# Later transposes, later gate products and a later start of v's preparation in a decoder step on one core

## The chip, the core and the metric

The kernel runs on one core of one Trainium2 chip. The metric is the device time of one execution in microseconds (us), as the median of several runs. The engines are TensorE (PE, with its weight loads PEld), VectorE (DVE), ScalarE (ACT), GpSimd (POOL) and SyncE (SP); the last three also issue DMAs.

## The reference, cut to what matters

One layer of a hybrid decoder works on 256 prompt tokens and 8 sample tokens, all in fp32. After two mixers and a norm (x1), 16384 experts of one neuron each are added (PEER). The change lies in this part:

```python
q = (xt @ w_q).reshape(n_pad, PEER_HEADS, 2, PEER_DKEY // 2)
s1 = einsum('thd,hkd->thk', q[:, :, 0], keys1); s2 = einsum('thd,hkd->thk', q[:, :, 1], keys2)
t1, i1 = top_k(s1, 16); t2, i2 = top_k(s2, 16)
cand = t1[..., :, None] + t2[..., None, :]           # 16 x 16 pairs of keys
top, pos = top_k(cand, 16)                           # 16 experts per head and token
gate = softmax(top)
hid = gelu(einsum('td,thkd->thk', xb, u_tab[ib]))    # u rows of the chosen experts
out = einsum('thk,thkd->td', gate * hid, v_tab[ib])  # v rows of the chosen experts
x2 = layer_norm(ALPHA * x1 + out)                    # then y = x2 + sigmoid(x2 @ wg) * (p @ wp)
```

## The kernel before

208 of the 264 tokens are treated densely: all 16384 neurons are computed for them as matrix products, and a gate matrix that is zero but for the chosen experts selects. The other 56 tokens are treated sparsely: the rows of their experts are gathered by indirect DMA (112 gathers of 128 rows, 1 MB each), and VectorE multiplies them with x1 (`ug`, L1365) or adds them up (`x1s`, L1375): these are called gather products here.

**The stages around the change.** The u stage makes the hidden values of 128 blocks of 128 experts (`pair_block` with `u_evac`, results to `a_d` in DRAM); the v stage makes 8 x 16 blocks that sum over the experts (`pair_block` with `v_evac`, sums in the tiles `acc`). A block is two *halves*; each half takes one half megabyte of weights. SyncE fetches them a block at a time into `w` (3 buffers), ScalarE rounds them to `whi` (L158), VectorE takes the rest `wlo` (L159), 5 buffers each, and TensorE multiplies by both: 16 matrix products in a half (L293 and L296 with `whi`, L294 with `wlo`).

**The order of the work.** The kernel writes its instructions out engine by engine from a small scheduler that runs while the program is built. After every half, `tick` is called once. It first runs functions that `defer(n, fn)` put n ticks later, and then the background tasks, which are generators: `yield x` spends x of the tick's budget, `yield ("w", n)` waits n ticks, and `Grid` keeps steps a fixed number of ticks apart. A tick has no length in time: it says only behind which half an instruction stands in its engine's queue. Each engine takes its queue in order. Halves and ticks are counted here from the start of the u stage; halves 0 to 255 are u, 256 to 511 are v.

**The tasks that the change touches.**
- `select_all`: chooses the experts for three groups of tokens (`select`, on VectorE, with the result `sel`: index parts and gates). For the two dense groups TensorE transposes `sel` into the bank `slt`, and ScalarE copies that into `slot`.
- `gates(t0, n)`: for four tokens a step, GpSimd (three tokens) and VectorE (one) make a one-hot row `o1` with the gate in it, and ScalarE makes `o2`. Six ticks later `g_mm` multiplies them on TensorE (bank `gps`, 4 products in fp32, eight records of the trace; called a gate product here) and ScalarE copies the result to the tile `gs`. Every eight steps, ScalarE's queue stores `gs` (2 MB) to `g_d` in DRAM. 20 steps belong to the first group, 32 to the second.
- `to_v`, called once when all gates are done and nothing is deferred: it closes the pools of selection and gates, opens the pool `vp` in the same memory, and spawns `prep(0)` and `residual`. `residual` copies x1 into the 16 tiles `acc` (ScalarE, two copies a tick). `prep(c)` makes the coefficients for one eighth of the v stage, in four parts: GpSimd's queue loads gates (`gl`) and hidden values (`al`), VectorE multiplies them (`al`, two instructions), ScalarE rounds (`co`), VectorE takes the rest (`co`). `gl` and `al` have two buffers. The v stage needs `prep(0)` done: the first half reads parts 0 and 1, the second parts 2 and 3.

In the program before, the first transposes stand behind half 53, the gate steps run from tick 55 to 210, `to_v` comes at tick 218, and the last gather product stands at tick 488. When sparse work is done, `folded` adds its last result (bank `yS`, 4 pieces on TensorE), and `Norm.rest` makes the sample part of the second norm beside the last eighth of v.

Of the kernel before, what the change touches and what calls it, by code (L numbers as in the profile page):

```python
# [18 lines left out]
PT = 256  # L19
# [26 lines left out]
NB, TR = divmod(TD, TB)  # L46
# [5 lines left out]
def hybrid_step(ctx: ExitStack, tc: tile.TileContext, xT, pT, w_in, w_dt, w_bs, w_bc, w_o, w_q, w_pg, w_pp,  # L52
                uT, vP, uR, vR, keysT, par, hpar, hist, h0, eye, tri, iota, fold, yT, o_hp, o_hs, o_cp, o_cs, o_sp, o_ss):
    nc = tc.nc
    te, ve, ac, gp, sy = nc.tensor, nc.vector, nc.scalar, nc.gpsimd, nc.sync
# [50 lines left out]
    def bank(name, tag="bg", bufs=4):  # L106
        return psum.tile([128, 512], F, name=name, tag=tag, bufs=bufs)
# [4 lines left out]
    ident = cpool.tile([128, 128], F, name="ident")  # L112
# [51 lines left out]
    tasks = []  # L164
    later = []
    clock = {"t": 0, "credit": 0.0, "in": False}

    def defer(n, fn):
        later.append((clock["t"] + n, fn))
# [33 lines left out]
    def spawn(gen, first=False):  # L203
        tk = {"gen": gen, "wait": 0}
        tasks.insert(0 if first else len(tasks), tk)
        return tk
# [864 lines left out]
    g_d = dram.tile([NB, 128, 128, TB], F, name="g_d")  # L1071
    gr_d = dram.tile([128, 128, TR], F, name="gr_d")
    DONE = {}
# [130 lines left out]
    def select_all():  # L1204
        while sum(h in DONE for h in range(PH)) < PH:
            yield ("w", 1)
        t2_stack.close()
        sp = P["sp"] = sp_stack.enter_context(tc.tile_pool(name="select", bufs=1))
        P["oh"] = oh_stack.enter_context(tc.tile_pool(name="onehot", bufs=1))
        for t, (t0, n, nh) in enumerate(TT):  # L1210
            sel = sp.tile([128, 3, nh * TOPK], F, name=f"sel{t}")
            yield from select(t, sel)
            if t < 2:
                send(sel, t, nh)
            if t == 1:
                spawn(sparse_experts(), True)
            if t != 1:
                nd = min(n, TD - t0)
                yield ("w", 2)
                ps = bank("slt")  # L1220
                for q in range(3):
                    te.transpose(ps[:, q * 128:q * 128 + n], sel[:n, q], ident[:n, :n])
                for q in range(3):
                    ac.copy(slot[q][:, t0:t0 + nd], ps[:, q * 128:q * 128 + nd])
                if t == 0:
                    tasks.insert(0, {"gen": gates(t0, nd), "wait": clock["t"] + 1})
        while "G" + str(PT // 2) not in DONE:
            yield ("w", 1)
        yield from gates(0, PT // 2)

# [27 lines left out]
    def gates(t0, n):  # L1258
        oh = P["oh"]
        grid = Grid()  # L1260
        for tt in range(t0, t0 + n, 4):
            b0, q0 = divmod(tt, TB)
            tb = TB if b0 < NB else TR
            if q0 == 0:
                GS["t"] = oh.tile([128, 128, TB], F, name="gs", tag="gs", bufs=2)
            gs = GS["t"].rearrange("p e t -> p (e t)")[:, 0:128 * tb].rearrange("p (e t) -> p e t", t=tb)
            o1 = oh.tile([128, 4, 128], F, name="o1", tag="o1", bufs=3)
            o2 = oh.tile([128, 4, 128], F, name="o2", tag="o2", bufs=3)
            for q in range(4):
                c = slice(tt + q, tt + q + 1)  # L1270
                (gp if q < 3 else ve).tensor_scalar(o1[:, q], iot, slot[0][:, c], slot[2][:, c], OP.is_equal, OP.mult)  # L1271
                ac.activation(o2[:, q], iot, AF.Abs, bias=slot[1][:, c], scale=-1.0)  # L1272
            ac.activation(o2, o2, AF.Relu, bias=1.0, scale=-1.0)
            defer(6, lambda o1=o1, o2=o2, gs=gs, q0=q0: g_mm(o1, o2, gs, q0))
            if q0 + 4 == tb:
                defer(8, lambda gs=gs, b0=b0: ac.dma_start(out=g_d[b0] if b0 < NB else gr_d, in_=gs))
            yield 0.1
            yield grid(3)
        DONE["G" + str(t0)] = True

    def g_mm(o1, o2, gs, q0):
        ps = bank("gps")
        for q in range(4):
            te.matmul(ps[:, q * 128:(q + 1) * 128], o2[:, q], o1[:, q], start=True, stop=True)  # L1284
        ac.copy(gs[:, :, q0:q0 + 4].rearrange("p e t -> p t e"), ps.rearrange("p (t e) -> p t e", e=128))
# [110 lines left out]
    ctx.push(oh_stack)  # L1396
    slot = [tp.tile([128, TD], F, name=f"slot{q}") for q in range(3)]
    spawn(select_all())


# [118 lines left out]
    def to_v():  # L1519
        nonlocal vp  # L1520
        oh_stack.close()
        sp_stack.close()
        tkp_stack.close()
        t1_stack.close()
        vp = ctx.enter_context(tc.tile_pool(name="vp", bufs=1))
        t = spawn(prep(0), True)
        spawn(residual())
        return t

    nxt = None  # L1530
    for e in range(NE):
        pair_block(x1_p, u_evac(e), 1.1)
        if nxt is None and "G0" in DONE and not later:
            nxt = to_v()
    while nxt is None:
        tick(1.2)
        if "G0" in DONE and not later:
            nxt = to_v()
    while len(ACC) < KB:
        tick(1.2)  # L1540
# [2 lines left out]
    for c in range(ECH):  # L1543
        run_out(nxt)
        if c + 1 < ECH:
            nxt = spawn(prep(c + 1), True)
# [151 lines left out]
```

## Time and profile before

| | us |
|---|---|
| median of 3 runs | 2490.54 (2488.34 to 2492.01) |
| the profiled execution | 2492.02 |
| its span, first to last instruction | 2490.2 |
| u stage (1076.6 to 1758.4) | 681.8 |
| v stage (1758.4 to 2374.5) | 616.1 |

Times in the profile count from the first instruction of the profiled execution. A row of the timeline is: start, duration, engine, line, operation, out<-in, shapes, count, and in brackets the idle time before it and what ended that. A row of the waits is: who <- what it waited for, total us, times, longest. A row of a group is: line, engine, operation, out<-in, shapes, count, then busy us, mean ns of one, and the idle time before them. A granted clock of 0.50 is half of TensorE's rate.

### The profile page before, as it was taken

What the parts mean: (1) busy time and instruction counts of PE and PEld (TensorE: products, weight loads), DVE (VectorE), ACT (ScalarE), POOL (GpSimd) and SP (SyncE); (2) the same over time, 40 slices, a digit from 0 to 9 for tenths busy, and PEclk for the clock granted to TensorE, in tenths of its full rate; (3) what the DMA queues carried; (4) which work ended last, traced back from release to release, by engine and by line L of the source; (5) the groups of instructions that cost most, each with busy time, mean ns of one, the idle gap of its engine ahead of it and who ended that gap; (6) DMA issues with size and microseconds to landing.
All of it is one profiled execution on the core that took longest, in us unless ns stands there. A gap on an engine that the chain in (4) does not pass through costs nothing.

```text
span 2490.2 us, 47970 instructions
## 1 busy us (share of the span) xinstructions
PE 2429.0 (98%) x19049; PEld 2403.0 (96%) x19049; DVE 2036.4 (82%) x3296; ACT 1424.4 (57%) x2206; POOL 626.2 (25%) x720
## 2 busy tenths in 40 slices
PE   8998999999999999999999999999999999999989
PEld 8998999999999999998999999999999999999989
DVE  7898976557455578999998777769899989999987
ACT  5656543455444455754677888866544555444564
POOL 2332200000000010100249567642332323322201
PEclk9999999999999999999999999999999999999999
DMA  6788855555555555566679999999999999999554
GB/s 223 245 280 264 284 203 177 199 188 201 189 201 189 201 188 198 198 206 206 227 277 356 371 371 363 361 358 395 392 380 386 383 375 395 374 371 376 192 176 148
DMA packets 137105, 688.91 MB, mean 277 GB/s; under 512 B 15744, under 2 KB 53168, under 8 KB 63280
## 3 DMA queue, kind: packets, MB, share of 16 engines
q1 hardware_dynamic: 89168, 495.46, 55.8%
q0 software_dynamic: 28688, 158.69, 16.4%
q10 hardware_dynamic: 19024, 31.69, 3.4%
q8 instruction: 149, 2.44, 0.4%
q14 instruction: 76, 0.62, 0.1%
HBM read 646.32 MB, written 39.46 MB: 275 GB/s over the span
## 4 chain that ended last, share of the span: by engine, by line
PE 61%; DVE 16%; DMA 10%; issue 7%; ACT 5%; POOL 1%; ACTq 0%; SPq 0%; DVEq 0%; POOLq 0%
PE mm L255 13%; PE mm L257 13%; PE mm L256 13%; PE mm L293 13%; DVE wlo L159 7%; PE mm L294 6%; DMA w<-vP 5%; ACT whi L158 2%; DMA w<-uT 2%; DVE ug L1365 1%; DMA h0t<-h 1%; PE gps L1284 1%; DVE acc L1482 1%; PE mm L296 1%; ACT o L1272 1%
## 5 line engine op out<-in xcount | busy, mean ns | idle before, releaser
L159 DVE TENSOR_TENSOR wlo<-w,whi 128x1024 fp32r<-128x1024 f32 x916 | 1112.6, 1223 | 336.3 <-ACT whi L158 327.9
L158 ACT CAST whi<-w 128x1024 fp32r<-128x1024 f32 x916 | 945.3, 1044 | 648.1 <-DMA w<-vP 228.6
L293 PE MATMUL mm<-x,whi 128*128 128x416 f32 x1920 | 573.1, 365 | 4.5 <-ACT whi L158 4.5
L293 PE MATMUL mm<-co,whi 128*128 128x416 f32 x1920 | 563.3, 362 | 0.0
L257 PE MATMUL mm<-x,wlo 128*128 128x264 f32 x1920 | 533.4, 278 | 12.4 <-DVE wlo L159 12.3
L255 PE MATMUL mm<-x,whi 128*128 128x264 f32 x1920 | 534.5, 278 | 4.7 <-ACT whi L158 4.7
L256 PE MATMUL mm<-x,whi 128*128 128x264 f32 x1920 | 531.9, 277 | 0.0
L294 PE MATMUL mm<-x,wlo 128*128 128x208 f32 x2048 | 504.6, 257 | 10.9 <-DVE wlo L159 10.8
L294 PE MATMUL mm<-co,wlo 128*128 128x208 f32 x2048 | 501.4, 255 | 6.5 <-DVE wlo L159 6.2
L294 PEld LDWEIGHTS mm<-x,wlo 128*128 128x128 f32 x2048 | 393.2, 193 | 18.9 <-DVE wlo L159 18.1
L294 PEld LDWEIGHTS mm<-co,wlo 128*128 128x128 f32 x2048 | 391.3, 192 | 10.9 <-DVE wlo L159 10.8
L257 PEld LDWEIGHTS mm<-x,wlo 128*128 128x128 f32 x1920 | 364.7, 190 | 15.1 <-DVE wlo L159 15.0
L293 PEld LDWEIGHTS mm<-x,whi 128*128 128x128 f32 x1920 | 365.9, 191 | 6.0 <-ACT whi L158 4.8
L255 PEld LDWEIGHTS mm<-x,whi 128*128 128x128 f32 x1920 | 364.9, 190 | 6.3 <-ACT whi L158 4.9
L256 PEld LDWEIGHTS mm<-x,whi 128*128 128x128 f32 x1920 | 364.9, 190 | 0.0
L293 PEld LDWEIGHTS mm<-co,whi 128*128 128x128 f32 x1920 | 364.0, 190 | 0.1
L1271 POOL TENSOR_SCALAR o<-iot,slot,slot 128x128 f32<-128x128 f32 x156 | 200.8, 1294 | 3.0 <-issue 1.2
L1295 POOL DMA_INDIRECT ug<-vR,sidx x56 | 105.2, 1879 | 271.8 <-DVE x1s L1375 212.8
L1295 POOL DMA_INDIRECT ug<-uR,sidx x56 | 94.7, 1691 | 247.1 <-DVE ug L1365 194.6
L1365 DVE SCALAR_TENSOR_TENSOR ug<-ug,x1s 128x2048 f32<-128x2048 f32 x56 | 127.8, 2283 | 2.3 <-DMA ug<-uR,sidx 2.3
L1375 DVE SCALAR_TENSOR_TENSOR x1s<-ug,scf,x1s 128x2048 f32<-128x2048 f32 x53 | 124.3, 2344 | 1.0 <-DMA ug<-vR,sidx 1.0
L898 POOL CAST r1h<-r1gbh 128x2 fp32r<-128x2 f32 x16 | 7.0, 439 | 439.9 <-DVE mxl L242 439.9
(364 smaller groups left out, 3927.1 us busy)
## 6 DMA issues: line engine op xcount, KB each, us to landing
w<-uT SPq DMA_DIRECT2D x128, 1024.0 KB
w<-vP SPq DMA_DIRECT2D x128, 1024.0 KB
w<-w_in SPq DMA_DIRECT2D x118, 1024.0 KB
w<-w_bc SPq DMA_DIRECT2D x16, 1024.0 KB
w<-w_bs SPq DMA_DIRECT2D x16, 1024.0 KB
w<-w_o SPq DMA_DIRECT2D x16, 1024.0 KB
w<-w_q SPq DMA_DIRECT2D x16, 1024.0 KB
w<-w_pg SPq DMA_DIRECT2D x16, 1024.0 KB
```

Source lines behind the costliest of these rows:

```text
L158: ac.copy(hi, w)
L159: ve.tensor_tensor(lo, w, hi.bitcast(F), OP.subtract)
L255: te.matmul(ps, wh, vh, start=(first and q == 0), stop=False)
L256: te.matmul(ps, wh, vl, start=False, stop=False)
L257: te.matmul(ps, wl, vh, start=False, stop=(last and q == n - 1))
L293: te.matmul(ps, hi[:, ws], both, start=(kb == 0), stop=False)
L294: te.matmul(ps[:, :TD], lo[:, ws], one, start=False, stop=False)
L296: te.matmul(ps, hi[:, ws], both, start=False, stop=True)
L1271: (gp if q < 3 else ve).tensor_scalar(o1[:, q], iot, slot[0][:, c], slot[2][:, c], OP.is_equal, OP.mult)
L1295: gp.indirect_dma_start(out=t, out_offset=None, in_=tab, in_offset=bass.IndirectOffsetOnAxis(ap=sidx[:, c:c + 1], axis=0))
L1365: ve.scalar_tensor_tensor(t, t, 1.0, x1s, OP.mult, OP.mult, accum_out=shid[:, c:c + 1])
L1375: ve.scalar_tensor_tensor(x1s, t, scf[:, c:c + 1], x1s, OP.mult, OP.add)
```

## The change

The transposes of `sel` and their copies become a deferred function, five ticks on, in place of a wait of two. The gates of the first group start six ticks after the selection instead of one after the transposes. Gate products are deferred by eight ticks instead of six, the stores by ten instead of eight. Of three steps, every third is four ticks from the next instead of three. And `to_v` waits until seven ticks have passed since gates and deferred work were done. By the scheduler's clock the gate steps now run from tick 58 to 230, the last store stands at tick 240, and `to_v` comes at tick 250, six halves before the end of u. 17 ticks then pass without a half, until `prep(0)` is done.

```diff
@@ select_all
-                yield ("w", 2)
-                ps = bank("slt")
-                for q in range(3):
-                    te.transpose(ps[:, q * 128:q * 128 + n], sel[:n, q], ident[:n, :n])
-                for q in range(3):
-                    ac.copy(slot[q][:, t0:t0 + nd], ps[:, q * 128:q * 128 + nd])
+
+                def to_slots(t0=t0, n=n, nd=nd, sel=sel):
+                    ps = bank("slt")
+                    for q in range(3):
+                        te.transpose(ps[:, q * 128:q * 128 + n], sel[:n, q], ident[:n, :n])
+                    for q in range(3):
+                        ac.copy(slot[q][:, t0:t0 + nd], ps[:, q * 128:q * 128 + nd])
+                    DONE["slot" + str(t0)] = True
+
+                defer(5, to_slots)
                 if t == 0:
-                    tasks.insert(0, {"gen": gates(t0, nd), "wait": clock["t"] + 1})
-        while "G" + str(PT // 2) not in DONE:
+                    tasks.insert(0, {"gen": gates(t0, nd), "wait": clock["t"] + 6})
+        while "G" + str(PT // 2) not in DONE or "slot0" not in DONE:
             yield ("w", 1)
@@ gates
-            defer(6, lambda o1=o1, o2=o2, gs=gs, q0=q0: g_mm(o1, o2, gs, q0))
+            defer(8, lambda o1=o1, o2=o2, gs=gs, q0=q0: g_mm(o1, o2, gs, q0))
             if q0 + 4 == tb:
-                defer(8, lambda gs=gs, b0=b0: ac.dma_start(out=g_d[b0] if b0 < NB else gr_d, in_=gs))
+                defer(10, lambda gs=gs, b0=b0: ac.dma_start(out=g_d[b0] if b0 < NB else gr_d, in_=gs))
             yield 0.1
-            yield grid(3)
+            yield grid(3 + (tt // 4 % 3 == 2))
@@ the u stage
+    def stored():
+        if "G0" in DONE and not later and "stored" not in DONE:
+            DONE["stored"] = clock["t"] + 7
+        return clock["t"] >= DONE.get("stored", 1 << 30)
+
     for e in range(NE):
         pair_block(x1_p, u_evac(e), 1.1)
-        if nxt is None and "G0" in DONE and not later:
+        if nxt is None and stored():
             nxt = to_v()
     while nxt is None:
         tick(1.2)
-        if "G0" in DONE and not later:
+        if stored():
             nxt = to_v()
```

On TensorE, the first transposes stood between halves 53 and 54 (the last products of a half, then `slt`, then the next half):

```order
L294 MATMUL mm<-x_12661,wlo_94 128x208
L293 MATMUL mm<-x_12661,whi_90 128x416
L294 MATMUL mm<-x_12661,wlo_94 128x208 x2
L296 MATMUL mm<-x_12661,whi_90 128x416
L1222 MATMUL slt<-ident,sel_14127 128x128 x3
L293 MATMUL mm<-x_12220,whi_13258 128x416
```

And now, three halves on:

```order
L293 MATMUL mm<-x_12367,whi_92 128x416
L294 MATMUL mm<-x_12367,wlo_95 128x208
L293 MATMUL mm<-x_12367,whi_92 128x416
L294 MATMUL mm<-x_12367,wlo_95 128x208
L1223 MATMUL slt<-ident,sel_14127 128x128 x3
L293 MATMUL mm<-x_12514,whi_91 128x416
```

TensorE has 48 more products ahead of the transposes than before, and the copies to `slot` on ScalarE move with them.

On ScalarE, before, the last store of the gates and the first copies of `residual` (`acc`), with the weights' `whi` between and behind them:

```order
L1276 DMA g_d<-gs 128x4096
L158 CAST whi_91<-w 128x1024
L158 CAST whi_90<-w 128x1024
L1409 COPY as<-mm 128x208
L1501 COPY acc<-x_12220 128x2x2x104 x2
L158 CAST whi_13258<-w 128x1024
```

Now the store stands here:

```order
L1289 COPY gs<-gps 128x4x128
L158 CAST whi_91<-w 128x1024
L158 CAST whi_90<-w 128x1024
L1413 COPY as<-mm 128x208
L1280 DMA g_d<-gs 128x4096
L158 CAST whi_13258<-w 128x1024
```

And the end of u, with the copies, is this:

```order
L158 CAST whi_13258<-w 128x1024
L1413 COPY as<-mm 128x208
L1417 ACTIVATE as<-as 128x416
L1418 DMA a_d<-as 128x416
L1459 CAST co<-al 128x8x104
L1505 COPY acc<-x_12367 128x2x2x104 x4
L1459 CAST co<-al 128x8x104
L1505 COPY acc<-x_12514 128x2x2x104 x4
L1459 CAST co<-al 128x8x104
```

Between store and first copies there were three instructions and are now some twenty, eleven halves' worth; and the last `co` stand behind the last u block's `as`, with no weights between.

On VectorE, before, `prep(0)` (`al`, `co`) stands among the weights of the u stage; a part of it:

```order
L1444 TENSOR_TENSOR al<-al,gl 128x4x192
L1445 TENSOR_TENSOR al<-al,gl 128x4x16
L159 TENSOR_TENSOR wlo_94<-w,whi_90 128x1024
L1375 SCALAR_TENSOR_TENSOR x1s<-ug,scf,x1s 128x2048
L159 TENSOR_TENSOR wlo_13259<-w,whi_13258 128x1024
L1410 TENSOR_TENSOR as<-mm,as 128x208
L159 TENSOR_TENSOR wlo_97<-w,whi_93 128x1024
L1456 TENSOR_TENSOR co<-al,co 128x8x104
```

Now, from the last u block's `as` on:

```order
L1414 TENSOR_TENSOR as<-mm,as 128x208
L1379 SCALAR_TENSOR_TENSOR x1s<-ug,scf,x1s 128x2048
L1460 TENSOR_TENSOR co<-al,co 128x8x104
L1379 SCALAR_TENSOR_TENSOR x1s<-ug,scf,x1s 128x2048
L1448 TENSOR_TENSOR al<-al,gl 128x4x192
L1449 TENSOR_TENSOR al<-al,gl 128x4x16
L1460 TENSOR_TENSOR co<-al,co 128x8x104
L1379 SCALAR_TENSOR_TENSOR x1s<-ug,scf,x1s 128x2048
L1448 TENSOR_TENSOR al<-al,gl 128x4x192
L1449 TENSOR_TENSOR al<-al,gl 128x4x16
L1460 TENSOR_TENSOR co<-al,co 128x8x104
L1379 SCALAR_TENSOR_TENSOR x1s<-ug,scf,x1s 128x2048
```

There is no `wlo` between them any more, and a gather product stands before each part; one more part and one more gather product follow, then the next `wlo`.

## The prediction

> **What bounds the kernel now.** I read the page first, then the busy time by stretches, the waits of TensorE, and the timelines of the few places where TensorE waits. The page says where to look.
>
> ```profile
> span 2490.2 us, 47970 instructions
> PE 2429.0 (98%) x19049; PEld 2403.0 (96%) x19049; DVE 2036.4 (82%) x3296; ACT 1424.4 (57%) x2206; POOL 626.2 (25%) x720
> ```
>
> TensorE is the bound, but its busy share is modelled, so I need a floor for a half-block (the kernel's tick) and compare stretches with it. The rows below are from one table by stretches: start:end, length, busy time and instructions of PE, PEld, DVE, ACT and POOL, then granted clock, DMA share, GB/s.
>
> ```profile
> 1076.60:1758.40 681.80, 661.36 (x4612) 650.57 (x4612) 580.79 (x986) 491.71 (x832) 309.73 (x238) 0.99 0.87 323
> 1758.40:2374.50 616.10, 607.56 (x4213) 602.83 (x4212) 574.38 (x625) 303.19 (x368) 183.09 (x186) 1.00 0.93 359
> 1968.50:1986.90 18.40, 18.40 (x129) 18.40 (x129) 18.40 (x20) 9.95 (x10) 5.38 (x5) 1.00 0.92 346
> 1466.10:1486.30 20.20, 20.20 (x145) 20.20 (x145) 14.30 (x16) 12.76 (x20) 14.95 (x10) 1.00 1.00 401
> 2175.90:2185.40 9.50, 9.50 (x74) 9.50 (x72) 9.37 (x11) 3.99 (x4) 2.13 (x2) 1.00 1.00 382
> ```
>
> The first two are the u stage and the v stage, 256 halves each. The third is eight halves with nothing beside them: 18.40 / 8 = 2.30 us, the floor. The fourth is eight halves with two gate products (16 extra records): (20.20 - 18.40) / 2 = 0.9 us per product, so 52 products are 47 us wherever they stand. The fifth is three halves with a piece of the experts' fold each: 9.50 / 3 - 2.30 = 0.87 us a piece. The u stage's floor is 256 x 2.30 + 47 = 636 of 682 us, the v stage's 589 of 616. What the change can win are those waits; what it can lose is a stretch in which TensorE has nothing to do. The waits of TensorE in the u stage from 1200 us on (total, times, longest):
>
> ```profile
> PE mm L294 <- DVE wlo L159: 6.5, 10, 1.8
> PE mm L293 <- ACT whi L158: 4.5, 1, 4.5
> PE gps L1284 <- POOL o L1271: 2.7, 2, 1.4
> PE slt L1222 <- DVE sel L1201: 2.4, 1, 2.4
> ```
>
> **Part 1, the transposes three halves later** (a wait of two ticks becomes a deferral of five). The stretch around the first transposes (halves 53 and 54), the clock just behind the wait, the last `sel`, and all that VectorE waits for in 1216 to 1272 us:
>
> ```profile
> 1214.30:1223.50 9.20, 6.82 (x38) 6.51 (x37) 8.22 (x18) 7.28 (x14) 3.01 (x5) 0.81 0.80 279
> 1219.40:1222.80 3.40, 3.40 (x13) 3.34 (x14) 2.53 (x4) 2.99 (x8) 2.31 (x5) 0.50 0.81 298
> 1219.04 0.29 DVE L1201 TENSOR_TENSOR sel<-sel,sm 128x128 f32<-128x128 f32 x1
> DVE wlo L159 <- ACT whi L158: 2.7, 2, 1.8
> ```
>
> Two halves and the transposes (about 0.35) need 4.95 us and took 9.20: 4.25 us lost, 2.4 in the wait for `sel` and the rest at half clock. With the transposes behind three more halves TensorE comes to them some 7 us after 1216.6 us, and `sel` is there at 1219.3: the wait goes. What is late next is VectorE: 2.7 us is all it waits there, so it is nearly full, and TensorE's lead can only be kept up to that. I take -2.7 (ends: 0, if `wlo` is the wait instead, and -4.25). The six evacuations and the second transposes move along on ScalarE and cost nothing new: nobody there waited for them.
>
> **Part 2, gate products two ticks later, steps 3, 3, 4 ticks apart.** The products are as many as before, so only waits count. GpSimd's group in 1313.7 to 1359.7 us:
>
> ```profile
> L1271 POOL TENSOR_SCALAR o<-iot,slot,slot 128x128 f32<-128x128 f32 x20 | 42.4, 2130 | 0.2
> L1295 POOL DMA_INDIRECT ug<-uR,sidx x5 | 9.7, 1936 | 0.8 <-DVE sel L1192 0.5 <-issue 0.3
> ```
>
> A step is 3 x 2.13 = 6.4 us there, and gathers (1.94 us each, every 3.5 ticks of some 2.6 us) take a fifth of GpSimd: 6.4 / 0.79 = 8.1 us a step against 3 ticks = 7.8 us before and 3.33 ticks = 8.7 us now. So GpSimd falls behind before and keeps up now, and the products come 5 us later besides: the 2.7 us of waits for `o` go. I take -2.7 (ends 0 and -3.4, with what the gaps cost around them). The stores of the gates to `g_d` go out two ticks later too; they are read first in the v preparation. Spread over 10 ticks per three steps, the gates end 20 ticks later (tick 233 of the stage instead of 213).
>
> **Part 3, v's preparation at tick 250 instead of 218.** Three things leave the u stage. First, the wait for the last store (ScalarE's timeline, then TensorE's halves 223 and 224 in the stretch table, and the clock behind):
>
> ```profile
> 1660.65 0.33 ACTq L1276 DMA_DIRECT2D g_d<-gs  x1
> 1676.93 1.01 ACT L1501 COPY acc<-x 128x416 f32<-128x416 f32 x2 [11.35 <-DMA g_d<-gs]
> 1671.90:1684.00 12.10, 7.04 (x34) 6.30 (x33) 3.53 (x4) 6.68 (x12) 5.22 (x7) 0.72 0.70 246
> 1678.90:1683.60 4.70, 4.14 (x13) 3.66 (x14) 3.12 (x4) 4.30 (x7) 3.76 (x6) 0.50 0.92 260
> ```
>
> The residual's copy lands in memory that the gates' tile held, so it waits till the store has landed, 16.3 us after its issue; `whi` stands behind it on ScalarE, and TensorE loses 12.10 - 2 x 2.30 = 7.5 us. Now the last store goes out at tick 240 and the copies come at 251, 11 x 2.30 = 25 us later: all 7.5 us go. Second, the first preparation's own stalls, and third, those of the v stage's beginning, where weights come late:
>
> ```profile
> 1700.40:1723.30 22.90, 21.39 (x147) 20.70 (x145) 20.75 (x21) 13.64 (x21) 5.95 (x6) 1.00 1.02 410
> 1776.80:1797.20 20.40, 19.01 (x130) 18.48 (x130) 18.86 (x20) 9.72 (x10) 6.11 (x7) 1.00 0.99 385
> ```
>
> Nine halves for 20.7 took 22.9 (-2.2); eight for 18.4 took 20.4 (-2.0), which a pause fills with weights, since SyncE can load two more tiles meanwhile. Together -4.2 (ends 0 and -6).
>
> The cost: `to_v` comes six halves before the u stage's end, and 17 ticks pass without a half. VectorE then works off, in this order and behind the last u block (time T): that block's sum, a gather product, `co`, a gather product, `al`, `co`, a gather product, `al`, `co`, a gather product, `al`, `co`. Their durations, from the groups of 1684 to 1723 us, with ScalarE's cast between `al` and `co`:
>
> ```profile
> L1375 DVE SCALAR_TENSOR_TENSOR x1s<-ug,scf,x1s 128x2048 f32<-128x2048 f32 x5 | 11.7, 2345 | 0.0
> L1444 DVE TENSOR_TENSOR al<-al,gl 128x768 f32<-128x768 f32 x3 | 2.9, 950 | 0.0
> L1410 DVE TENSOR_TENSOR as<-mm,as 128x208 f32<-128x208 f32 x7 | 2.6, 367 | 0.0
> L1456 DVE TENSOR_TENSOR co<-al,co 128x832 fp32r<-128x832 f32 x2 | 2.1, 1026 | 0.6 <-ACT co L1455 0.6
> L1445 DVE TENSOR_TENSOR al<-al,gl 128x64 f32<-128x64 f32 x3 | 0.7, 220 | 0.0
> L1455 ACT CAST co<-al x32: 948/982/1012, 1693.9 to 2268.5; 128x832 fp32r<-128x832 f32 x32
> ```
>
> That is 0.37 + 4 x 2.35 + 4 x 1.03 + 3 x (0.95 + 0.22 + 0.98) = 20.3 us (the first cast lies beside a gather product). TensorE takes the first half's first quarter at T + 4, waits for the next `co` each time, and finishes the last quarter of the second half at T + 20.3 + 1.15 = T + 21.5, where without a pause it would be at T + 4.6: 16.9 us lost. It comes back at half clock: the 0.50 row above lasted 4.7 us after the store's wait, and the one in the tail, behind a wait of 4.9 us, 5.6 us:
>
> ```profile
> PE mm L1561 <- DVE acc L1482: 7.2, 2, 4.9
> 2384.50:2390.10 5.60, 5.53 (x25) 5.54 (x26) 3.88 (x8) 2.89 (x8) 0.54 (x3) 0.50 0.54 189
> ```
>
> Half of some 5 us is 2.5, so the pause costs +19.4. The Trainium skill (TensorE: Matmul & The Clock Gate, Part 1) says that the clock halves after an idle window of about 3.4 us and is full again after about 3.4 us of sustained work; by that the loss would be 1.7 and the whole sum 0.8 lower. The rows agree on the half, and on a longer way back. Ends: 14, if gather products wait their turn behind `co` less than I think, and 25, if the loads land late (below).
>
> What the pause does is not lost on VectorE: about 4.5 gather products are done in it, so the experts end 24 halves earlier (position 473 of 512 instead of 497). That takes three products out of the last eighth of the v stage, and it moves four pieces of the last fold before it.
>
> ```profile
> 2288.90:2384.50 95.60, 83.68 (x568) 81.34 (x566) 87.99 (x134) 49.57 (x85) 25.65 (x49) 0.96 0.62 220
> 2372.21 0.58 DVE L1482 TENSOR_TENSOR acc<-mm,acc 128x416 f32<-128x416 f32 x1
> 2376.93 1.23 DVE L159 TENSOR_TENSOR wlo<-w,whi 128x1024 fp32r<-128x1024 f32 x1 [0.85 <-ACT whi L158]
> 2378.07 0.58 DVE L1482 TENSOR_TENSOR acc<-mm,acc 128x416 f32<-128x416 f32 x1
> ```
>
> This eighth is VectorE's (88 of 95.6 us), so three products less are -7.0. But when the second norm's sample part runs, the engines turn in a ring: one block per 2378.07 - 2372.21 = 5.86 us instead of 4.60, with about 1.05 us of VectorE's time idle in each. In the changed order that part begins six blocks earlier, and some five more turns cost +5.2. The fold's four pieces now stand where TensorE is the bound: 4 x 0.87 = +3.5. Sum of the last eighth: +1.7 (ends -7 and +5).
>
> **Sum**: +19.4 - 2.7 - 2.7 - 7.5 - 4.2 + 1.7 = +4.0 us. The profiled execution took 2492.0 us (2490.2 between first and last instruction, 1.8 around it), 1.5 over the median of 2490.5; so 2496.0 for it, and 2494.5 against the median.
>
> **Rivals.** (1) Slower by more: the loads for the third and fourth part of the first preparation can only go out when `co` frees a buffer, 4 and 10 us behind T, and behind a gather on GpSimd's queue. GpSimd and VectorE before:
>
> ```profile
> 1696.51 0.54 POOL L1431 DMA_DIRECT2D al<-a_d  x1 [0.60 <-DVE co L1456]
> 1704.92 0.95 DVE L1444 TENSOR_TENSOR al<-al,gl 128x768 f32<-128x768 f32 x1
> ```
>
> There 8.4 us pass between the issue and the use. I have some 6 us for it in the pause, and count on queues that are emptier once the weights' buffers are full. If they land only after 8.4 us, each of the two adds about 2.5: +9, 2500. It decides when a load takes over 6 us. (2) VectorE eats parts 1 and 2. It is busy for 134.5 of 145 us around them, small gaps between its instructions not counted:
>
> ```profile
> 1158.60:1303.60 145.00, 135.75 (x916) 131.51 (x916) 134.53 (x317) 97.76 (x163) 39.21 (x40) 0.98 0.70 243
> ```
>
> So the waits for `sel` and `o` come back as waits for `wlo`. Then 5.4 us of the gains go: +9.4, 2500. (3) Faster: the pause is shorter and the ring is no longer than before. With 14 for the pause, -7 + 3.5 for the last eighth and the full ends of parts 1 and 2 (-7.6), it comes to 14 - 7.6 - 7.5 - 4.2 - 3.5 = -8.8, 2482. For it speaks that the v stage after the pause has fewer gathers to share its DMA engines (0.93 busy) with; against it, that VectorE's chain in the pause has no part that can run elsewhere. (4) The change does not do what it says, the copy still waiting for a store: excluded by 25 against 16.3 us, unless stores land 9 us later than before.
>
> **Chances.** The forecast case, within 0.2% (5 us, about what a measurement of this kernel can tell from no change): 0.39. Rival 1 0.20, rival 2 0.12, together 0.32 slower. Rival 3 0.29 faster. The range reaches to both: 2482 to 2503 (rivals 1 and 2 together are beyond it).
>
> **What the changed profile would show.** Right: no wait of `slt` and `gps` in TensorE's waits, no wait of `acc` on ScalarE, and one pause of 17 to 25 us between the last `mm<-x` and the first full half of `mm<-co`, granted clock 0.5 in it; the last eighth at 91 to 98 us. Wrong: more than 8 us waiting for `wlo` before 1380 us, `al` waiting for its DMA in the pause, or a last eighth under 90 us. The sum stands on two large terms of opposite sign, the pause and the store's wait; an error of a fifth in the first alone moves the result out of its band.

## The result and the profile after

| | before | after |
|---|---|---|
| median | 2489.72 us (2487.4 to 2496.0, 6 runs) | 2514.34 us (2508.73 to 2516.86, 6 runs) |
| the profiled execution, its span | 2492.02, 2490.2 | 2516.86, 2515.1 |

The ratio is 1.0092, with a 95% interval of 1.0078 to 1.0106: slower by 0.9%, some 23 us, where +4 was forecast. The profiled executions differ by 24.9 us; the changed kernel's was the slowest of its six, 2.5 us over their median. First the page of the changed kernel, then the table by stretches: the u stage, the pause (from the last product of half 255 to the first of half 258, found from the starts of the halves), the rest of the v stage, and the last eighth with the wait behind it.

```profile
span 2515.1 us, 47953 instructions
PE 2433.0 (97%) x19049; PEld 2401.8 (95%) x19049; DVE 2038.6 (81%) x3296; ACT 1424.5 (57%) x2206; POOL 642.0 (26%) x720
1073.80:1749.50 675.70, 657.33 (x4611) 647.24 (x4610) 575.35 (x976) 481.44 (x817) 331.32 (x231) 1.00 0.87 322
1749.50:1782.10 32.60, 10.32 (x35) 8.82 (x34) 22.67 (x23) 13.95 (x22) 9.35 (x10) 0.55 0.94 360
1782.10:2399.00 616.90, 605.56 (x4181) 596.91 (x4180) 559.50 (x616) 299.90 (x362) 169.23 (x181) 1.00 0.90 343
2314.90:2409.00 94.10, 81.19 (x535) 75.95 (x533) 78.79 (x127) 50.46 (x85) 17.61 (x47) 0.98 0.54 182
```

Two halves in the pause have a floor of 4.6 us and took 32.6: 28.0 us lost, at a granted clock of 0.55. The u stage is only 6.1 us shorter than before (675.7 against 681.8), and the v stage without its two halves in the pause is longer than the whole of it was. The waits of TensorE, from 1200 us to the end of u and then to the end of v:

```profile
PE mm L294 <- DVE wlo L159: 9.1, 14, 1.2
PE mm L293 <- ACT whi L158: 2.9, 1, 2.9
PE x1t L1329 <- ACT x1s L1319: 1.8, 1, 1.8
...
PE mm L293 <- DVE co L1460: 13.7, 3, 8.3
PE mm L294 <- DVE wlo L159: 10.5, 16, 1.4
PE mm L293 <- issue: 8.5, 1, 8.5
```

No `slt`, no `gps`: the waits that parts 1 and 2 aimed at are gone. ScalarE no longer waits for the store with `acc` either, but in this execution the store still costs. It was issued at 1707.02; ScalarE's rows behind it, and the two halves 245 and 246:

```profile
1707.02 0.33 ACTq L1280 DMA_DIRECT2D g_d<-gs  x1
1713.70 1.05 ACT L158 CAST whi<-w 128x1024 fp32r<-128x1024 f32 x1 [4.70 <-DMA w<-uT]
1722.62 1.99 ACT L158 CAST whi<-w 128x1024 fp32r<-128x1024 f32 x2 [5.74 <-DMA w<-uT]
1718.30:1728.80 10.50, 6.75 (x34) 6.17 (x33) 4.80 (x5) 3.32 (x5) 0.94 (x1) 0.84 1.01 415
```

The weights wait for DMA engines that are full (share 1.01, 415 GB/s), and two halves take 10.5 us instead of 4.6: 5.9 us lost, where ScalarE's wait had cost 7.5. This price is not a fixed one. In nogather (below), whose queues are the same up to `to_v` and whose store goes out whole at 1707.25, ScalarE waits for weights for 13.0 us from 1700 to 1740 us, against 18.5 here, and TensorE does not wait at all. The same stretch there:

```profile
1718.30:1728.80 10.50, 10.50 (x75) 10.38 (x74) 5.79 (x7) 4.52 (x6) 1.77 (x2) 1.00 0.96 400
```

Then the pause, with the end of u at T = 1749.5. VectorE's last `as`, and each `al` and `co` that TensorE waits for; GpSimd's load for the second part of `prep(0)`; TensorE's first products of the first two parts:

```profile
1754.60 0.37 DVE L1414 TENSOR_TENSOR as<-mm,as 128x208 f32<-128x208 f32 x1
1757.15 1.02 DVE L1460 TENSOR_TENSOR co<-al,co 128x832 fp32r<-128x832 f32 x1
1765.95 0.96 DVE L1448 TENSOR_TENSOR al<-al,gl 128x768 f32<-128x768 f32 x1 [5.47 <-DMA al<-a_d]
1768.04 1.02 DVE L1460 TENSOR_TENSOR co<-al,co 128x832 fp32r<-128x832 f32 x1 [0.99 <-ACT co L1459]
1773.32 1.03 DVE L1460 TENSOR_TENSOR co<-al,co 128x832 fp32r<-128x832 f32 x1 [0.99 <-ACT co L1459]
1778.60 1.02 DVE L1460 TENSOR_TENSOR co<-al,co 128x832 fp32r<-128x832 f32 x1 [0.99 <-ACT co L1459]
...
1748.54 0.61 POOL L1435 DMA_DIRECT2D al<-a_d  x1
...
1758.26 0.69 PE L293 MATMUL mm<-co,whi 128*128 128x416 f32 x1 [8.54 <-issue]
1769.12 0.72 PE L293 MATMUL mm<-co,whi 128*128 128x416 f32 x1 [8.31 <-DVE co L1460]
```

The last three `co` are 5.28 us apart, where the prediction's terms give 5.53 (product, `al`, cast, `co`). But the chain ends at 1779.6, T + 30.1 instead of T + 20.3. The 9.8 us are in its first links. By the prediction's durations the second part's `al` was due at T + 6.1. It came at T + 16.5, having waited 5.47 us for a load that was issued at 1748.5 and is used 17 us later. The last `as` was late too, at T + 5.1 and not at T; but `al` had to wait for the load in any case, so here the load decided. The kernel before shows that `as` as late, at T + 5.7 (T = 1758.4 there):

```profile
1764.14 0.37 DVE L1410 TENSOR_TENSOR as<-mm,as 128x208 f32<-128x208 f32 x1
```

DMA by three stretches (start:end, length, busy PE, PEld, DVE, ACT, POOL, clock, DMA share, GB/s), and how long a load of `al` took from issue to landing in the first (two loads, 11.9 and 17.3 us; the row has the middle) and in the third of them:

```profile
1735.90:1749.50 13.60, 13.60 (x97) 13.57 (x95) 12.36 (x13) 8.62 (x14) 5.14 (x6) 1.00 1.01 411
1749.50:1766.00 16.50, 2.77 (x10) 2.15 (x8) 9.55 (x11) 5.57 (x9) 4.49 (x5) 0.59 1.02 410
1766.00:1782.00 16.00, 7.45 (x24) 6.58 (x25) 13.03 (x13) 8.38 (x13) 4.86 (x5) 0.50 0.87 308
...
al<-a_d POOLq DMA_DIRECT2D x2, 416.0 KB, 14.6
al<-a_d POOLq DMA_DIRECT2D x1, 416.0 KB, 6.1
```

With TensorE standing, the engines still moved 410 GB/s for 16.5 us, while the weights' buffers were refilled. In the third stretch the weights' queue moved nothing, and only there does a load take the 6 us that the prediction counted on. The Trainium skill (DMA: Bandwidth & Descriptors, Queues, rings and completion order) says that each DMA engine takes turns between the queues that have work, packet by packet; 6.1 us with the weights' queue idle and 14.6 with it busy agree with that.

### The profile page after: what moved, and what is told of

It is laid out like the page before. It is cut to its first block, busy times and chain, and to the rows that moved or that the text cites. A ratio compares the mean times of both kernels' runs of the same rounds, so it can differ in the third digit from the quotient of the medians.

```text
span 2515.1 us, 47953 instructions
## 1 busy us (share of the span) xinstructions
PE 2433.0 (97%) x19049; PEld 2401.8 (95%) x19049; DVE 2038.6 (81%) x3296; ACT 1424.5 (57%) x2206; POOL 642.0 (26%) x720
## 4 chain that ended last, share of the span: by engine, by line
PE 56%; DVE 17%; DMA 14%; issue 6%; ACT 6%; POOL 1%; ACTq 0%; SPq 0%; DVEq 0%; POOLq 0%
PE mm L255 12%; PE mm L257 12%; PE mm L256 12%; PE mm L293 10%; DVE wlo L159 7%; DMA w<-vP 5%; PE mm L294 5%; DMA w<-uT 4%; ACT whi L158 3%; DMA al<-a_d 2%; DVE x1s L1379 1%; DMA h0t<-h 1%; DVE ug L1369 1%; ACT o L1276 1%; DMA ug<-vR,sidx 1%
## 5 line engine op out<-in xcount | busy, mean ns | idle before, releaser
L294 PE MATMUL mm<-co,wlo 128*128 128x208 f32 x2048 | 504.7, 257 | 11.3 <-DVE wlo L159 10.5
L257 PEld LDWEIGHTS mm<-x,wlo 128*128 128x128 f32 x1920 | 364.1, 190 | 17.1 <-DVE wlo L159 17.0
L1275 POOL TENSOR_SCALAR o<-iot,slot,slot 128x128 f32<-128x128 f32 x156 | 232.4, 1495 | 5.9 <-ACT slot L1225 3.1
L1299 POOL DMA_INDIRECT ug<-vR,sidx x56 | 96.4, 1721 | 265.3 <-DVE x1s L1379 204.7
```

What stands on the lines that cost most here:

```text
L257: te.matmul(ps, wl, vh, start=False, stop=(last and q == n - 1))
L294: te.matmul(ps[:, :TD], lo[:, ws], one, start=False, stop=False)
L1299: gp.indirect_dma_start(out=t, out_offset=None, in_=tab, in_offset=bass.IndirectOffsetOnAxis(ap=sidx[:, c:c + 1], axis=0))
```

## The experiments

Each ratio is against the kernel before, on the same chip, over five rounds. The places come from one profiled execution each, which can lie some 5 us from its kernel's median; so the times decide, and the traces say where. Line numbers in an experiment's rows are those of its own kernel. This table gives the start of a half against the same half before, both counted from their half 0 (us, negative is ahead), from the traces:

| half | after | p1only | p2only | p3only | plus0 |
|---|---|---|---|---|---|
| 60 | -3.6 | -2.5 | -0.1 | 0.1 | -2.5 |
| 104 | -7.7 | -4.1 | -4.2 | -1.4 | -7.7 |
| 221 | -6.8 | 0.9 | 2.9 | 1.0 | -3.6 |
| 226 | -12.5 | -6.5 | -2.1 | -6.5 | -9.9 |
| 242 | -11.7 | -2.7 | -2.2 | -5.9 | -9.1 |
| 254 | -6.0 | -0.8 | 1.4 | -5.7 | -7.8 |
| 258 | 21.9 | -0.8 | 16.7 | -5.7 | 13.1 |
| 480 | 28.8 | 3.2 | 25.7 | -4.7 | 19.1 |
| 511 | 27.4 | 0.5 | 25.3 | -5.4 | 17.9 |

Between halves 221 and 226 stands the wait for the store in the kernel before; a version that has it elsewhere gains there and can lose it again at its own place.

The leads up to half 226 do not compare like work: a version that makes its gate products later has made fewer by then. By half 104 the trace has 15 of the 52 in the kernel before, 11 in the changed kernel and plus0, 14 in p1only and 13 in p2only; by half 221 it has 52 before, 47 in the changed kernel and plus0, and 48 in p2only. At 0.9 us a product, 4.5 of the changed kernel's 6.8 us at half 221 are work put off, and 2.3 us are won. From half 242 on, all have made 52.

### The parts, one at a time

p1only is the first hunk of the change alone (`to_slots`, the gates' start and the wait for `slot0`). p2only is the hunk in `gates`, p3only is `stored()`, and plus0 is the whole change with

```diff
-            DONE["stored"] = clock["t"] + 7
+            DONE["stored"] = clock["t"] + 0
```

> Part 1 alone; gate products, stores and to_v keep their rules, so to_v comes at tick 222 and prep(0) still ends ahead of half 256. Border theory (what the changed kernel loses is lost at the border of u and v, by the parts of prep(0) that stand behind the last half of u, while parts 1 and 2 gain by themselves): the 4.2 us at halves 53 and 54 stay gained and no pause comes: -3.5 us against before, about 2486. Transfer theory (the DMA engines, 0.93 to 0.99 busy from 1390 us on, are the real bound, so that any wait removed comes back as late weights a few halves on): no change, within 1 us of before.

> Part 2 alone: to_v at tick 238, two parts of prep(0) behind the last half of u, ten ticks without a half. The copies of residual stand right behind the last store again, so its wait (7.5 us) stays. Border theory: part 2's 2.7 us are gained, and VectorE works off two gather products, two co and one al (about 9 us) behind the end of u, which holds the second v half up by 5.6 us, and 2 us of half clock: +5 us against before, about 2495. Transfer theory: no gain from part 2, and late loads in the pause: +10, about 2500.

> Part 3 alone: gates and their stores as before (last store at tick 218), to_v eight ticks later (226), prep(0) still issued ahead of half 256 but for nothing; two ticks without a half. The copies of residual come some 20 us behind the store, which took 16.3 us to land, so its wait of 7.5 us goes. Border theory: no pause, the store makes weights late by some us at most: -4 us against before (ends -7.5 and -1.5), about 2486.5. Transfer theory: the wait comes back in full as late weights: within 1 us of before, or up to +2.

> Parts 1 and 2 without the seven ticks of part 3: to_v at tick 242, nine ticks without a half instead of 17, two to three parts of prep(0) behind the last half of u, and the wait for the last store back (7.5 us, in place of the 6 us of late weights at halves 245 and 246). Border theory: the chain of VectorE behind the end of u has three gather products, three co and two al, about 14.5 us, so TensorE loses 11 and 2.5 at half clock instead of 28: -13 us against the changed kernel, about 2502, +11 against before. Transfer theory: the loss hangs on the full DMA engines and not on the seven ticks: within 4 us of the changed kernel.

Part 1 alone: 2487.89 us, 0.9983 (0.9973 to 0.9994), faster by a little, as the border theory had it; of the 4.1 us at half 104 its trace keeps none at half 221, so how much of part 1 lasts is not settled by place.

Part 2 alone: 2513.30 us, 1.0081 (1.0062 to 1.0100). Both theories missed it, by 18 and 13 us. Two parts of `prep(0)` behind the end of u (T = 1757.5 here) cost 15.3 us in halves 256 and 257 alone, and not 7.6. VectorE's last `as` and the two `co`, and TensorE's waits there:

```profile
1766.36 0.37 DVE L1410 TENSOR_TENSOR as<-mm,as 128x208 f32<-128x208 f32 x1
1768.67 1.03 DVE L1456 TENSOR_TENSOR co<-al,co 128x832 fp32r<-128x832 f32 x1 [1.94 <-ACT co L1455]
1773.95 1.03 DVE L1456 TENSOR_TENSOR co<-al,co 128x832 fp32r<-128x832 f32 x1 [0.99 <-ACT co L1455]
...
PE mm L293 <- DVE co L1456: 11.3, 2, 8.6
```

From that `as` on the chain is no longer than was counted (a product, two `co` and an `al`), but it begins 8.9 us behind T, since VectorE still had weights, an `al` and a product to do when TensorE was through. So in this trace it is not the number of parts behind the border but VectorE's backlog at it. Another 9.0 us are lost between halves 258 and 480; why was not tried. plus0 came to 2508.07 us, 1.0076 (1.0057 to 1.0095), with 20.9 us lost in the two halves where 13.5 were expected. Beside the 1.0092 of the changed kernel its seven ticks less are worth some 4 us, the transfer theory's bound, and the intervals hardly tell that from none. The store's wait, expected back, is there on ScalarE (5.0 us) and costs TensorE nothing.

Part 3 alone: 2489.66 us, 1.0003 (0.9990 to 1.0016). Its trace has the store's wait gone and no pause, and 5 us ahead to the end; its times say no change. That was left open, and is taken up below.

### What sets the length of the pause

hold keeps gather products and gathers back while the scheduler waits for `prep(0)` behind u:

```diff
             yield grid(STEP - (i % (4 if vp else 2) == 0))
+            while "pause" in DONE:
+                yield ("w", 1)
             t = rows.pop(i)
...
+    DONE["pause"] = True
     while len(ACC) < KB:
         tick(1.2)
...
         run_out(nxt)
+        DONE.pop("pause", None)
```

early issues the second load of `prep(0)` right behind the first:

```diff
                 load(k)
+                if c == 0:
+                    load(k + 1)
                 yield ("w", 4)
-            if k % 4 < 3:
+            if k % 4 < 3 and k + 1 not in AL:
                 load(k + 1)
```

split4 cuts the last store in four:

```diff
-                defer(10, lambda gs=gs, b0=b0: ac.dma_start(out=g_d[b0] if b0 < NB else gr_d, in_=gs))
+                if tt != PT // 2 - 4:
+                    defer(10, lambda gs=gs, b0=b0: ac.dma_start(out=g_d[b0] if b0 < NB else gr_d, in_=gs))
+                else:
+                    for e in range(0, 128, 32):
+                        defer(10 + e // 16, lambda gs=gs, b0=b0, e=e: ac.dma_start(out=g_d[b0, :, e:e + 32], in_=gs[:, e:e + 32]))
...
-            DONE["stored"] = clock["t"] + 7
+            DONE["stored"] = clock["t"] + 3
```

> The changed kernel, with no gather products and no new gathers while the scheduler waits for prep(0) behind the last half of u (they resume with the v stage; the fold then comes at half 482 instead of 473). VectorE theory (the prediction's: the pause is the chain of VectorE, four gather products among the parts): the pause loses four products, 28.0 - 9.4 = 18.6 us, and the kernel comes to about -9 us against the changed one, 2505. Load theory (the pause is as long as the loads take, each of which can only be issued when a buffer of al comes free, and then needs 8 to 17 us): the loads pace the parts, the pause keeps 24 to 28 us: -2 us (0 to -4), 2512.

> The changed kernel, with the load of the second part of prep(0) issued right behind the first (tick 251 instead of 255, some 11 us sooner on GpSimd); nothing else moves. Load theory: the 5.5 us wait of al for its DMA in the pause goes, if the next load (issued when the first al is free) then lands within 7 us of its issue; else a part of it comes back there: -4 us (-5.5 to -1) against the changed kernel, about 2510. VectorE theory: the wait lies beside work that the chain must do in any case: no change, 2514.

> The changed kernel, with the last 2 MB store of the gates cut into four of 0.5 MB, issued at ticks 240, 242, 244 and 246 instead of all at 240; to_v stays at tick 250. Burst theory (one store of 2 MB put on the queues at once holds back the weights, which costs the 6 us at halves 245 and 246): those 6 us shrink to 2 or less, -4 us, about 2510. Volume theory (the DMA engines are full with what must move, in whatever order, and lateness only builds up): the same 6 us are lost, spread over halves 245 to 252, and the loads behind them land later: within 1 us of the changed kernel, or +3.

hold came to 2512.38 us, 1.0081 (1.0063 to 1.0099), as the load theory had it; the pause lost 25.2 us. Three of the four products were out of the pause. Products taken out of VectorE's chain only turned into waiting for the load:

```profile
1757.53 1.02 DVE L1462 TENSOR_TENSOR co<-al,co 128x832 fp32r<-128x832 f32 x1
1766.36 0.96 DVE L1450 TENSOR_TENSOR al<-al,gl 128x768 f32<-128x768 f32 x1 [7.81 <-DMA al<-a_d]
```

early came to 2518.17 us, 1.0104 (1.0087 to 1.0121): no gain, against the load theory's -4. Its interval holds the changed kernel's 1.0092, so the VectorE theory's "no change" is met by number, but not by its reason. The wait of `al` is gone, but a gather product ahead of the first `co` now waits for its own transfer, and the pause lost 29.8 us:

```profile
1761.38 2.35 DVE L1379 SCALAR_TENSOR_TENSOR x1s<-ug,scf,x1s 128x2048 f32<-128x2048 f32 x1 [5.19 <-DMA ug<-vR,sidx]
1763.64 1.02 DVE L1462 TENSOR_TENSOR co<-al,co 128x832 fp32r<-128x832 f32 x1
```

So neither the chain alone nor that one load alone is the bound: whatever is issued last before 1750 us lands at 1761 to 1766. split4 came to 2512.30 us, 1.0092 (1.0075 to 1.0110). In its trace halves 245 and 246 run at the floor (11.0 us ahead at half 242, 11.3 at half 254). But nogather runs them at the floor with the store in one piece, so this does not show that the cut did it. The pause lost 30.6, and in the sum the volume theory's number is right: nothing gained.

A third theory was formed from these: the transfers share full engines. nogather takes transfers away; it is hold, with the mark set in `to_v` and a second wait ahead of `get(i + 1)`:

```diff
+            while "pause" in DONE:
+                yield ("w", 1)
             get(i + 1)
...
         nonlocal vp
+        DONE["pause"] = True
```

> The changed kernel, with no gathers and no gather products from to_v (tick 250) until the v stage begins; they come later, so that the fold stands at half 497, as in the kernel before. In the run that held them from tick 256 on, al still waited until 1766 us for its second load. Sharing theory (the loads of prep(0) land late since the DMA engines, full at 410 GB/s from 1736 to 1766 us, must also bring 3 to 4 gathers of 1 MB and refill the weights' buffers): without the gathers some 8 us of transfers are gone, the second load lands 5 to 8 us sooner, the pause costs about 18 us instead of 25 to 28, and the kernel comes to about 2502. Latency theory (a load takes its 14 to 17 us whatever else moves): the pause stays at 24 us or more, 2509 or more.

It came to 2501.79 us, 1.0044 (1.0027 to 1.0061). The sharing theory said 2502. T is 1743.9 here; `al` for the second and third part, and the stretch from T on:

```profile
1753.76 0.95 DVE L1452 TENSOR_TENSOR al<-al,gl 128x768 f32<-128x768 f32 x1
1760.93 0.96 DVE L1452 TENSOR_TENSOR al<-al,gl 128x768 f32<-128x768 f32 x1 [3.49 <-DMA al<-a_d]
1743.90:1760.90 17.00, 5.34 (x18) 4.30 (x16) 8.21 (x11) 10.47 (x19) 3.85 (x6) 0.58 0.95 335
```

The second part's `al` comes at T + 9.9, without a wait, where it came at T + 16.5; the engines carry 335 GB/s instead of 410. The pause lost 21.0 us (18 were expected: the third load waits too, since it can only be issued when `co` has freed a buffer). The edit does three things at once, so the 7 us are not all the engines' sharing: the gathers are off the engines, four gather products are out of VectorE's chain, and the second load goes out at 1732.1 instead of 1748.5, since no gather stands before it in GpSimd's queue. hold shows that fewer products alone gain at most 2.8 us in the pause, and early that an earlier issue alone gains none. The third load compares better. GpSimd's row of its issue, and the row of the changed kernel's third load, which was issued at 1760.40 among gathers:

```profile
1754.13 0.54 POOL L1439 DMA_DIRECT2D al<-a_d  x1 [2.99 <-DVE co L1464]
al<-a_d POOLq DMA_DIRECT2D x1, 416.0 KB, 10.5
```

With no gather in flight it was there 6.8 us after its issue, at 1760.93, and not after 10.5. So the loads were late because of what moved beside them. How much of that falls to the gathers and how much to the weights was not tried apart.

### Can the store's wait be had for nothing?

resdelay leaves everything of the kernel before where it is, but for the copies that wait:

```diff
     def residual():
+        yield ("w", 8)
         for db in range(KB):
...
-        spawn(residual())
+        spawn(residual(), True)
```

p1res is the same with part 1, and p12res with part 1, part 2's deferrals of 8 and 10 and steps of three. best1 is parts 1 and 3 with `spawn(residual(), True)`. p3res is the kernel before with part 3 and `spawn(residual(), True)`, and best3 is best1 with three ticks instead of seven in `stored()`.

> A candidate to beat both kernels: part 1 and part 3 without part 2 (gate products and stores as before, steps of three ticks), and residual ahead of the other background tasks, so that its copies are done in eight ticks and nothing waits for them at the end of u. to_v at tick 230, the fourth part of prep(0) at tick 253, three ticks without a half instead of 17. Border theory: part 1 gives 4, the store's wait 7.5, late weights behind the store take back up to 6, the last part of prep(0) holds the second half of v up by 0 to 5 us: -5 us against before (-9 to +1), about 2486. Transfer theory: no change, 2491.

> The kernel before with one edit: residual begins eight ticks after to_v, and ahead of the other tasks; prep(0), gates and stores stay where they were. ScalarE then has no wait for the last store (7.5 us at halves 223 and 224), and nothing of prep(0) moves toward the end of u. Border theory: the store's wait goes, and late weights behind the store take back 0 to 4: -5 us against before, about 2487. Transfer theory (weights late behind the store in any case): within 1 us of before, 2492.

> Part 1 together with a residual that begins eight ticks after to_v (tick 222) and ahead of the other tasks. Part 1 alone measured 0.998 of before. Border theory: both gains add: -8 us against before, about 2484. Transfer theory: the second gain does not show: as part 1 alone, 2488.

> Part 1, the deferrals of part 2 (gate products 8 ticks later, stores 10) with steps of three ticks throughout, and a residual that begins eight ticks after to_v (tick 222) and ahead of the other tasks. prep(0) ends at tick 248 or so, and no tick passes without a half. Border theory: part 1 and the store's wait, and what the later gate products add: -9 us against before, about 2483. Transfer theory: the gate products' gain is taken back by late weights: as with steps of three and deferrals of six, 2484 to 2488.

> The kernel before, with part 3 (to_v at tick 226 instead of 218) and residual ahead of the other background tasks; gates and stores as before, no tick without a half, the fold at half 497. Loads and copies both come behind the last store's landing here, where the residual's delay alone left the loads of prep(0) behind the store, and VectorE waited 9.8 us for them. Store theory (the wait goes only when everything that needs the store, the loads as well as the copies, stands far enough behind it): no wait of more than 2 us in halves 220 to 240, -5 us against before, about 2488. Transfer theory (the 2 MB hold back the weights by as much in any case): within 1 us of before, 2493.

> Part 1, to_v three ticks after the gates' last deferred work (tick 226 instead of 222), and residual ahead of the other background tasks; gate products, stores and steps as before, no tick without a half, the fold at half 497. Store theory: part 1 (0.998 of before alone) and the store's wait add: -8 us against before, 2485, as good as part 1 with the delayed residual (0.9975) or better. Transfer theory: as part 1 alone, 2488. Border theory's limit: the last part of prep(0) stands at tick 250, six halves ahead of its use; if that is too near, co is waited for at half 257 as in the run with to_v at 230 (5 us lost there).

| | to_v at tick | median, us | ratio to before (95%) |
|---|---|---|---|
| best1 | 230 | 2498.14 | 1.0025 (1.0013 to 1.0038) |
| resdelay | 218 | 2493.15 | 1.0005 (0.9993 to 1.0017) |
| p12res | 222 | 2488.96 | 0.9988 (0.9975 to 1.0000) |
| p3res | 226 | 2488.11 | 0.9979 (0.9967 to 0.9991) |
| p1res | 222 | 2485.06 | 0.9975 (0.9963 to 0.9988) |
| best3 | 226 | 2485.86 | 0.9968 (0.9953 to 0.9982) |

resdelay gains nothing: the transfer theory's number, by another way than it named. ScalarE no longer waits for the store, and GpSimd and VectorE do. The first load must not read `g_d` before the store has landed: it goes out at 1679.04, 17.1 us behind the store's issue, and `al` stands ahead of the weights in VectorE's queue. GpSimd's row of resdelay, the same row of p1only (which names the store), VectorE's of resdelay, and there TensorE's only wait from 1660 to 1700 us:

```profile
1679.04 0.93 POOL L1428 DMA_DIRECT2D gl<-g_d  x1 [18.32 <-issue]
1682.50 0.92 POOL L1432 DMA_DIRECT2D gl<-g_d  x1 [16.93 <-DMA g_d<-gs]
1688.64 0.96 DVE L1444 TENSOR_TENSOR al<-al,gl 128x768 f32<-128x768 f32 x1 [9.76 <-DMA al<-a_d]
PE mm L294 <- DVE wlo L159: 6.9, 1, 6.9
```

7.5 us on ScalarE became 6.9 on VectorE. In p3res loads and copies both stand behind the landing and no tick passes without a half, and the waits of TensorE are small, from 1660 to 1800 us:

```profile
PE mm L294 <- DVE wlo L159: 4.8, 7, 1.1
PE mm L293 <- ACT whi L158: 0.6, 1, 0.6
```

It is faster by 0.2%, which the store theory had (2488 expected, 2488.11 measured); its trace is 5.4 us ahead at half 226 and only 0.4 at half 511. Of the 5.8 us by which its span is shorter, 5.5 lie ahead of half 0, where the kernels are the same. So the gain is shown by the times, and its place is not shown. The difference between p3only and p3res is the two ticks without a half and what follows from them; that this is why p3only shows no gain was not tried by itself.

best1, which both theories had too fast, shows how near the border is: with `to_v` at 230 the second half of v waits 3.8 us for the last `co`, and with the half clock behind it halves 257 and 258 lose 6.9 us.

```profile
PE mm L293 <- DVE co L1460: 3.8, 1, 3.8
```

With `to_v` at 226 (best3) that row is gone, and the kernel is 0.3% faster than before and, by the two ratios, 1.2% faster than the changed one. p1res (2485.06 of 2484 expected) is as good within the intervals; since resdelay by itself gave nothing, it is not shown that p1res has more than part 1. p12res, 2488.96 where the border theory had 2483, shows no gain from gate products two ticks later.

## Why the prediction was wrong

Direction and size were wrong: same was forecast, with slower at 0.32, and 2514 lies beyond the range. By the prediction's own terms, with the measured ones from the table of leads and 0.9 us a gate product:

| step | forecast, us | measured, us |
|---|---|---|
| parts 1 and 2, up to half 221, less the five gate products still to come | -5.4 | -2.3 |
| store's wait and the first preparation's stalls, halves 221 to 242, without these five | -9.7 | -9.4 |
| late weights behind the moved store, halves 242 to 254 | 0 | +5.7 |
| the pause, halves 254 to 258 | +19.4 | +27.9 |
| halves 258 to 480: v's start, four pieces of the fold | +1.5 | +6.9 |
| halves 480 to 511: three products less, ring | -1.8 | -1.4 |
| before half 0 and behind half 511 | 0 | -2.5 |
| sum | +4.0 | +24.9 |

**Parts 1 and 2** did only in part what was counted. No wait for `sel` or `o` is left, but of 5.4 us only 2.3 are kept at half 221. From 1200 to 1660 us TensorE's waits for `wlo` went from 7 with 4.4 us to 13 with 8.3 us. That is rival 2 (VectorE eats the gain), at a part of its price; its sign, over 8 us of these waits before 1380 us, did not come (4.4). In the five other traces whose queues are the same up to there (plus0, hold, early, split4, nogather), the lead at like work lies between 1.8 us ahead and 0.8 behind.

**The store** is the first step that failed. The wait itself went, with the first preparation's stalls (9.4 of 9.7 us). But "all 7.5 us go" counted one waiter, and put what the store does at its new place at nothing. 5.7 us came back there as late weights in the profiled execution; 3.5 in hold, 4.9 in early, none in nogather. So the size is not settled. resdelay shows a further payer: the loads that read what was stored, and behind them VectorE.

**The pause** is the second, and the largest miss. The length of a turn of the chain was right to 0.25 us; the time of its start was not. The step "I have some 6 us for it in the pause, and count on queues that are emptier once the weights' buffers are full" failed: the weights' queue was at work until about T + 16, and the second load took 17.3 us. Rival 1 had the mechanism, but put it at the third and fourth load and priced it at 5 us. It struck at the second load, which was issued ahead of T. The chain ended 9.8 us later than counted; the half clock took 1.3 us from the pause (its last 2.5 us, the last quarter at a clock of 0.50, were counted as 1.15) and not 2.5. Together that is the 8.5 us. hold shows that the load and not the products set the length; by nogather, the load is late because of the transfers beside it. The prediction's own sign for it ("`al` waiting for its DMA in the pause") is in the profile.

**v's start** is the third. The fold's 3.5 us are there, 24 halves earlier as forecast (its last pieces at halves 468 to 471 instead of 492 to 495). The gain of 2.0 from weights loaded in the pause is not seen: up to the last eighth TensorE's waits for `wlo` in v come to 5.4 us (8 waits) and not 3.7 (7). What sets their number was not tried, and that does not account for all of the 5.4 us missed here; across the runs this stretch varies by several us, and the cause stays open.

**The last eighth** was right in its sum: 94.1 us stood in a forecast of 91 to 98. The three products less are there, and VectorE has 78.8 instead of 88.0 us, 9.2 less where 7.0 were counted; what the ring's further turns cost was not measured by itself.

## What to carry to other kernels

A wait for a transfer is not gone when its waiter is moved. Ask who else waits for the same bytes, in which queue, and what those bytes displace on engines that are near full. A pause of the bounding engine does not drain the others: their backlog (weights ahead of the needed piece in VectorE's queue, refills on the DMA engines) runs first, and a load that took 6 us with the weights' queue idle took 17. So work for the next stage is best issued early enough to end ahead of the border. In this kernel, moving it eight ticks later, with the copies ahead of the other tasks, gained 0.2%, and moving it by 32 in the whole change lost 0.9%. And compare leads only where the same work is done: most of the 6.8 us at half 221 was work put off.

## What the runs showed of the hardware

The DMA engines carried 410 to 415 GB/s at a share of 1.01 to 1.02 whether TensorE ran or stood (the changed kernel's rows of 1718.3, 1735.9 and 1749.5 us). The same 416 KB load landed after 11.9 and 17.3 us among gathers and weights, after 10.5 us toward the end of the weights' refill, and after 6.1 us when the weights' queue was idle. A 2 MB store in one piece cost TensorE 5.9 us in one execution and nothing in another with the same queues up to there (the two rows of 1718.3 us).
